# A joined set of new orders in a two-layer decoder trunk: paired u blocks, split first loads, gate products moved, and wide SwiGLU products first

## The chip, the cores and the metric

The kernel runs on one core of one Trainium2 chip. The metric is device time in microseconds for one execution, as the median of several. Five engines work side by side: TensorE (PE in the profile; its weight loads are PEld), VectorE (DVE), ScalarE (ACT), GpSimd (POOL) and SyncE (SP), whose queue issues nearly all loads.

## The reference

Sequence 256, model width 1024, two layers, all in float32. Layer 0 mixes tokens with a gated MLP, layer 1 with an mLSTM. Each mixer is followed by a SwiGLU and by a gated embedding.

```python
def gmlp_mixer(x, w_in, ln_g, ln_b, w_s, b_s, w_out):
    z = jax.nn.gelu(x @ w_in)                 # 1024 -> 2 x 3072
    u, v = jnp.split(z, 2, axis=-1)
    v = layer_norm(v, ln_g, ln_b)             # over 3072, then in 8 groups
    sv = jnp.einsum('gts,bcsgd->bctgd', ws, v) + b_s.T[:, :, None]
    return (u * sv.reshape(B, S, GM_HALF)) @ w_out

def mlstm_mixer(x, ...):
    xm, z = jnp.split(x @ w_in, 2, axis=-1)   # 1024 -> 2 x 2048
    xc = jax.nn.silu(causal_depthwise_conv(xm, conv_w, conv_b))
    q, k, v = (headwise_linear(a, w) for a, w in ((xc, w_q), (xc, w_k), (xm, w_v)))
    gates = jnp.concatenate([q, k, v], axis=-1) @ w_gates + b_gates
    h = mlstm_cell(...)                       # 4 heads of 512, stabilised by running maxima
    h = layer_norm(h, norm_g).reshape(B, S, ML_INNER) + skip * xc
    return (h * jax.nn.silu(z)) @ w_out

def swiglu(x, w_gate, w_up, w_down):          # 1024 -> 2816 -> 1024
    return (jax.nn.silu(x @ w_gate) * (x @ w_up)) @ w_down

for i in range(DEPTH):
    x = layer_norm(ALPHA * x + mixer_i(x), ln1_g[i], ln1_b[i])
    x = layer_norm(ALPHA * x + swiglu(x, ...), ln2_g[i], ln2_b[i])
    x = x + sigmoid(x @ ple_w_gate[i] + ple_b_gate[i]) * (p[i] @ ple_w_proj[i])
```

## The kernel before, in words

**Every product is three.** A float32 operand is split into a high part (a cast to float32r, on ACT) and a low part (the difference, on DVE; both by `split`, L150). A product is then high by high, high by low and low by high. Two forms exist. In the plain form (`mm_feat`, L242, used by `feat_from_x`, L247) a block of 128 features takes 24 products of 256 columns, three per slice of the model width. In the paired form (`feat_pair`, L252) the high and low parts of x stand side by side in `xs`, so one product of 512 columns (a *wide* one) does two of the three, and one of 256 columns (a *narrow* one) the third: eight wide, then eight narrow. A paired result lies in two halves of a PSUM bank, which `pair_sum` (L259) adds: a copy on ACT, then an add on DVE. Before the change the SwiGLU's gate and up blocks are paired, and the gMLP's u blocks and the mLSTM's xm and z blocks are plain.

**Weights.** All weights pass through one list (`weight_plan`, L74) in the order of their use. `weight(...)` (L205) hands out the next one and calls `ahead` (L169), which lets SP load up to 8 weights ahead into four `raw` buffers and casts up to 4 ahead into six `w` buffers (or, for those in `WIDE`, eight `b8` buffers). `EARLY` (L50) names weights that are put into the list next to another one, ahead of their turn, among them the embedding's gates (`pg`) beside blocks of the down projection (`d`). Reading a `w` buffer on TensorE frees it for the cast six later.

**PSUM.** Two pools of four banks: A for accumulators, scores and gates, B for blocks in passing.

**The stages.** Four pairs of loads of x and of the v weights open the program (L342 to L363), with seven warm-up products on TensorE meanwhile. Then come the gMLP's v (six column groups of 512), its u and sv blocks with the output projection three steps behind (L465 to L477), the boundary with layer norm, the SwiGLU (`gate_up`, L529, blocks 4 to 21; the down projection two blocks behind), the boundary and the embedding. Layer 1 follows: in a loop over 16 feature blocks (L770) `xm_block` makes the convolution, `qv_block` q and v, and `s_block` the scores. Then the gate chain (L785 to L840) turns accumulated gate values into exponents. Small transposes on TensorE (`gp`, `cp`) and a broadcast (`gb`) feed a chain of narrow DVE and ACT operations, with z blocks 8 to 11 between. `pv_block` (L844) multiplies scores by values for each head, normalises each head by its own statistics (`num`, `pd`, and the scale by `rsqrt` on POOL) and writes `hn`; z blocks 12 to 15 lie between the heads. `h_block` (L882) transposes `hn` and multiplies by z. The output projection (`Down`, L280; weights `mo`) accumulates into all four A banks: `acc.add` does both token halves of a block, but the last four blocks' second halves are held for the boundary.

The scheduler orders the instructions of each engine from the program's order and its own estimates; each engine then runs its row strictly in order.

## Time and profile before

| | |
|---|---|
| median of 3 runs | 838.34 us (837.59 to 840.28) |
| the profiled execution's own time | 837.17 us |
| its span in the profile | 835.4 us |
| TensorE busy | 824.1 us (99%), 4727 products |
| DVE busy | 608.8 us (73%) |
| ACT busy | 472.5 us (57%) |
| POOL busy | 158.4 us (19%) |
| read from memory | 153.67 MB, 185 GB/s over the span |

In rows of the timeline the first number is the start in microseconds, the second the length, then engine, line, operation, output and inputs by the program's names, partitions by elements, and the count. In brackets stands how long the engine had been idle before it, and what released it. Matmuls are pipelined: neighbours overlap, so the pace of TensorE is read from the differences of starts and not from the lengths.

### The profile page before, as it was taken

The numbers are of one execution on the slowest core, as the hardware profiler recorded it, in microseconds if no ns is written. First come the engines' busy times: TensorE is split into PE (matmuls) and PEld (weight loads), VectorE is DVE, ScalarE is ACT, GpSimd is POOL, SyncE is SP. The second block draws the span as 40 slices with busy tenths as digits, with TensorE's granted clock in tenths as the row PEclk, the third lists the DMA queues.
The fourth block names the chain that finished last, engine by engine and source line by source line (L and its number), as shares of the span: only waits on it lengthen the run. The fifth ranks groups of instructions, "written<-read, shape, count | busy, mean of one in ns | idle before, by whom it ended". The sixth has DMA issues, their size and how long they took to land.

```text
span 835.4 us, 12743 instructions
## 1 busy us (share of the span) xinstructions
PE 824.1 (99%) x4727; PEld 719.6 (86%) x4727; DVE 608.8 (73%) x933; ACT 472.5 (57%) x803; POOL 158.4 (19%) x222
## 2 busy tenths in 40 slices
PE   8999999999999999999999999999999999999997
PEld 5889999998888888888889999898878888888886
DVE  6667996567856666578878998578886666677684
ACT  6556665555544555467347787685544555566522
POOL 1021654443100001800101655230010000000010
PEclk9999999999999999999999999999999999999999
DMA  8885465567286655588234444253646655577601
GB/s 299 294 304 178 143 196 192 177 196 243 102 290 202 188 191 193 164 261 265 80 134 165 140 140 154 95 193 121 209 166 243 206 190 193 187 244 259 202 0 52
DMA packets 44710, 155.55 MB, mean 186 GB/s; under 512 B 5224, under 2 KB 5992, under 8 KB 44648
## 3 DMA queue, kind: packets, MB, share of 16 engines
q1 hardware_dynamic: 44360, 154.47, 56.0%
q8 instruction: 37, 0.61, 0.3%
q10 hardware_dynamic: 288, 0.26, 0.1%
q14 instruction: 25, 0.20, 0.1%
HBM read 153.67 MB, written 1.05 MB: 185 GB/s over the span
## 4 chain that ended last, share of the span: by engine, by line
PE 63%; DVE 5%; DMA 3%; ACT 2%; issue 1%; POOL 1%; DVEq 0%; ACTq 0%; SPq 0%; POOLq 0%
PE pu L255 8%; PE pg L255 8%; PE acc L239 5%; PE acc L238 5%; PE acc L240 5%; PE pu L257 4%; PE pg L257 4%; PE gate L275 2%; PE gate L278 2%; PE gate L276 2%; PE first L275 2%; PE first L278 2%; PE first L276 2%; DVE w L152 2%; DMA raw<-in_ml_wo 1%; PE xmps L243 1%
## 5 line engine op out<-in xcount | busy, mean ns | idle before, releaser
L152 DVE TENSOR_TENSOR w<-raw,w 128x1024 fp32r<-128x1024 f32 (+1 forms) x277 | 337.2, 1225 | 108.6 <-ACT w L152 106.0
L152 ACT CAST w<-raw 128x1024 fp32r<-128x1024 f32 (+1 forms) x276 | 287.3, 1045 | 152.7 <-PE acc L240 50.7
L238 PE MATMUL acc<-w,h 128*128 128x512 f32 x336 | 132.0, 393 | 1.6 <-ACT hn L878 1.0
L239 PE MATMUL acc<-w,h 128*128 128x512 f32 x336 | 131.5, 391 | 0.0
L240 PE MATMUL acc<-w,h 128*128 128x512 f32 x336 | 130.8, 390 | 0.5 <-DVE w L152 0.5
L238 PEld LDWEIGHTS acc<-w,h 128*128 128x128 f32 x336 | 63.2, 188 | 14.5 <-ACT hn L878 1.4
L240 PEld LDWEIGHTS acc<-w,h 128*128 128x128 f32 x336 | 63.1, 188 | 14.5 <-DVE w L152 1.0
L239 PEld LDWEIGHTS acc<-w,h 128*128 128x128 f32 x336 | 63.2, 188 | 11.1 <-DVE h L152 0.3
L255 PE MATMUL pu<-xs,w 128*128 128x512 f32 x288 | 72.3, 393 | 0.0
L255 PE MATMUL pg<-xs,w 128*128 128x512 f32 x288 | 71.8, 391 | 0.0
L255 PEld LDWEIGHTS pg<-xs,w 128*128 128x128 f32 x288 | 53.8, 188 | 11.0
L307 POOL TENSOR_SCALAR ve<-mv 128x1 f32<-128x1 f32 x8 | 6.1, 758 | 294.8 <-DVE mv L327 290.5
L255 PEld LDWEIGHTS pu<-xs,w 128*128 128x128 f32 x288 | 51.5, 188 | 9.3
L244 PE MATMUL ups<-xs,w 128*128 128x256 f32 x192 | 53.7, 280 | 0.0
L243 PE MATMUL ups<-xs,w 128*128 128x256 f32 x192 | 53.6, 279 | 0.0
L245 PE MATMUL ups<-xs,w 128*128 128x256 f32 x192 | 53.6, 279 | 0.0
L442 POOL TENSOR_TENSOR sv<-sv,cf 128x256 f32<-128x256 f32 x24 | 31.1, 1298 | 67.8 <-ACT sv L441 64.0
L257 PEld LDWEIGHTS pg<-xs,w 128*128 128x128 f32 x288 | 38.9, 188 | 3.1
L257 PEld LDWEIGHTS pu<-xs,w 128*128 128x128 f32 x288 | 38.9, 188 | 3.1
L257 PE MATMUL pu<-xs,w 128*128 128x256 f32 x288 | 39.5, 279 | 0.0
L257 PE MATMUL pg<-xs,w 128*128 128x256 f32 x288 | 39.4, 279 | 0.0
L238 PE MATMUL vps<-w,xs 128*128 128x512 f32 x96 | 37.6, 392 | 1.5 <-ACT w L152 0.8
(240 smaller groups left out, 1675.7 us busy)
## 6 DMA issues: line engine op xcount, KB each, us to landing
raw<-in_ffn_g SPq DMA_DIRECT2D x44, 512.0 KB, 3.9
raw<-in_ffn_u SPq DMA_DIRECT2D x44, 512.0 KB, 4.0
raw<-in_ffn_d SPq DMA_DIRECT2D x44, 512.0 KB, 3.4
raw<-in_gm_u SPq DMA_DIRECT2D x24, 512.0 KB, 3.5
raw<-in_gm_wo SPq DMA_DIRECT2D x24, 512.0 KB, 3.4
raw<-in_gm_v SPq DMA_DIRECT2D x23, 512.0 KB, 4.9
raw<-in_ple_gate SPq DMA_DIRECT2D x16, 512.0 KB, 4.5
raw<-in_ml_z SPq DMA_DIRECT2D x16, 512.0 KB, 3.3
```

The costliest lines, as they stand in the source:

```text
L152: return dve.tensor_copy(hi, src) if fast else act.copy(hi, src), sub.tensor_tensor(lo, src, hi.bitcast(F32), ALU.subtract)
L238: pe.matmul(ps, lh, w[:, 0, c], start=start, stop=False)
L239: pe.matmul(ps, ll, w[:, 0, c], start=False, stop=False)
L240: pe.matmul(ps, lh, w[:, 1, c], start=False, stop=stop)
L243: pe.matmul(ps, w[:, 0, c], h, start=start, stop=False)
L244: pe.matmul(ps, w[:, 0, c], l, start=False, stop=False)
L245: pe.matmul(ps, w[:, 1, c], h, start=False, stop=stop)
L255: pe.matmul(ps, w[:, 0, k * P:(k + 1) * P], xs[:, k], start=k == 0, stop=False)
L257: pe.matmul(ps[:, 0], w[:, 1, k * P:(k + 1) * P], xh[:, k, :], start=False, stop=k == KD - 1)
L275: pe.matmul(ps, xh[:, k, TOK[t]], w[:, 0, c], start=k == 0, stop=False)
L276: pe.matmul(ps, xh[:, k, TOK[t]], w[:, 1, c], start=False, stop=False)
L278: pe.matmul(ps, xl[:, k, TOK[t]], w[:, 0, c], start=False, stop=k == KD - 1)
```

## The change

It joins several edits.

- *Start.* The first three v weights (before: the first alone) are loaded and cast in halves. The second half of the first x tile is issued by SP behind the first half weight, not by ACT. Eight warm-up products instead of seven.
- *u blocks.* They take the paired form, with `pair_sum` ahead of the Gelu.
- *SwiGLU.* `feat_pair` is cut in two. In all but the last two blocks the wide products of both factors come first, then the narrow ones of both.
- *Embedding gates.* The early casts of `pg` lie beside down blocks 10 to 15 instead of 13 to 18.
- *xm blocks.* The split of xm comes ahead of the three convolution steps on DVE.
- *Gate chain.* The gate transposes lie within z block 8 (after three of its eight slices), the transposes `cp` and all broadcasts `gb` within z block 10, in two banks. z block 12 is done there too, and one activation covers five blocks.
- *Heads.* The square of the reciprocal is taken early, and the variance's scale and the epsilon are one DVE operation; one POOL operation goes. Four weights are cast ahead of the last head. z blocks 13 to 15 follow heads 0 to 2, and none follows head 3.
- *Output projection.* Blocks 0 and 1 do their first token halves one after the other, then their second halves.

```diff
-WARM = 7
+WARM = 8
...
+LAST = 2
+GATES_STEP = 3
...
-EARLY |= {("d", l, 13 + k): ("pg", l, k) for l in range(2) for k in range(6)}
+EARLY |= {("d", l, 10 + k): ("pg", l, k) for l in range(2) for k in range(6)}
...
-    return key[0] in ("g", "u") and len(key) == 3 and key[-1] >= 4
+    return key[0] in ("g", "u") and len(key) == 3 and key[-1] >= 4 or key[0] == "u" and len(key) == 2
...
-            for c in HALF if at["load"] == 0 else [slice(0, n)]:
+            for c in HALF if at["load"] < 3 else [slice(0, n)]:
                 sp.dma_start(t[:, c], ap[:, c])
+                if at["load"] == 0 and c.start == 0:
+                    second_x()
...
-                for c in () if key[0] == "bdv" else HALF if i == 0 else [slice(0, n)]:
+                for c in () if key[0] == "bdv" else HALF if i < 3 else [slice(0, n)]:
...
-    def feat_pair(ps, w):
+    def feat_pair_high(ps, w):
 
         for k in range(KD):
             pe.matmul(ps, w[:, 0, k * P:(k + 1) * P], xs[:, k], start=k == 0, stop=False)
+
+    def feat_pair_low(ps, w):
         for k in range(KD):
             pe.matmul(ps[:, 0], w[:, 1, k * P:(k + 1) * P], xh[:, k, :], start=False, stop=k == KD - 1)
...
     def u_block(f):
-        ps = bank("B", [P, S], "ups")
-        feat_from_x(ps, weight("u", f))
+        ps = bank("B", [P, 2, S], "ups")
+        feat_pair(ps, weight("u", f))
         us[f] = tl("s", [P, S], name="u")
-        act.activation(us[f], ps, AF.Gelu_apprx_tanh)
+        pair_sum(us[f], ps)
+        act.activation(us[f], us[f], AF.Gelu_apprx_tanh)
...
-            pg = bank("B", [P, 2, S], "pg")
-            feat_pair(pg, weight("g", l, f))
+            pg, pu = bank("B", [P, 2, S], "pg"), bank("B", [P, 2, S], "pu")
+            wg = weight("g", l, f)
+            feat_pair_high(pg, wg)
+            if f < NF - LAST:
+
+                wu = weight("u", l, f)
+                feat_pair_high(pu, wu)
+                feat_pair_low(pg, wg)
+            else:
+                feat_pair_low(pg, wg)
+                wu = weight("u", l, f)
+                feat_pair_high(pu, wu)
             pair_sum(s, pg)
             act.activation(s, s, AF.Silu)
-            pu = bank("B", [P, 2, S], "pu")
-            feat_pair(pu, weight("u", l, f))
+            feat_pair_low(pu, wu)
             pair_sum(y, pu)
...
-            act.activation(y, ps, AF.Identity, bias=par[:, f, 4:5], scale=par[:, f, 3:4])
-            for j in (1, 2, 3):
-                dve.scalar_tensor_tensor(y[:, j:], ps[:, :S - j], par[:, f, 3 - j:4 - j], y[:, j:], ALU.mult, ALU.add)
...
+            act.activation(y, ps, AF.Identity, bias=par[:, f, 4:5], scale=par[:, f, 3:4])
             split(xm[0][:, 0, :], xm[0][:, 1, :], ps)
+            for j in (1, 2, 3):
+                dve.scalar_tensor_tensor(y[:, j:], ps[:, :S - j], par[:, f, 3 - j:4 - j], y[:, j:], ALU.mult, ALU.add)
...
-            z8 = z_mm(8)
...
+            z8 = z_mm(8, (GATES_STEP, transpose_gates))
...
+            gbs = [bank("A", [P, 2, 2, P], "gb") for _ in range(2)]
+            z = z_mm(10, (GATES_STEP, transpose_cols))
...
-            act.activation(sz[1][:, 0:4, :], sz[1][:, 0:4, :], AF.Silu)
+            z_copy(*z_mm(12))
+            act.activation(sz[1][:, 0:5, :], sz[1][:, 0:5, :], AF.Silu)
...
-            dve.tensor_tensor(rs, mv[:, :, 1], dn, ALU.mult)
-            dve.tensor_tensor(rs, rs, dn, ALU.mult)
-            rsqrt(rs, rs, 2)
+            for t in range(2):
+                dve.tensor_scalar(rs[:, t:t + 1], mv[:, t, 1:2], dn2[:, t:t + 1], EPS, ALU.mult, ALU.add)
+            pool.tensor_tensor(rs, rs, mhalf[:, :2], ALU.pow)
...
+            if h == NH - 1:
+                ahead(LOAD_AHEAD, 4)
             pv_block(h)
-            z_act(*z_mm(12 + h))
+            if h < NH - 1:
+                z_act(*z_mm(13 + h))
...
-                acc.add(f, hs.pop(f), weight("mo", f, casts=1 if f >= NI - 2 else None))
+                block = (f, hs.pop(f), weight("mo", f, casts=1 if f >= NI - 2 else None))
+                if f == 0:
+                    first = block
+                elif f == 1:
+
+                    for t in range(2):
+                        for b, h2, w in (first, block):
+                            acc.mm(b, t, h2, w)
+                else:
+                    acc.add(*block)
```

`transpose_gates` and `transpose_cols` hold the transposes that stood in line before, and the second also the four `gb` products; `feat_from_x` calls them after three slices.

More of the change, by code (lines that the diff above doesn't have):

```diff
@@ L350, in trunk @@
         if i == 0:
-            for k in range(2):
-                act.dma_start(t[:, k, :], a["xT"][i, :, k, :])
+            act.dma_start(t[:, 0, :], a["xT"][i, :, 0, :])
+            second_x = lambda: sp.dma_start(xr[0][:, 1, :], a["xT"][0, :, 1, :])
+            xr.append(t)
         else:
             sp.dma_start(t, a["xT"][i])
+            xr.append(t)
         ahead(1 + i, int(i == 0))
-        xr.append(t)
     make_identity(nc, ident)
@@ L687, in transpose_z, with z_mm @@
                 act.copy(sz[0][:, 0:4, TOK[t]], tp)
-        def z_mm(f):
+        def z_mm(f, between=(None, None)):
             ps = bank("B", [P, S], "zps")
-            feat_from_x(ps, weight("z", f, casts=2 if f > 10 else None))
+            feat_from_x(ps, weight("z", f, casts=2 if f > 10 else None), between)
             return f, ps
@@ L794, in mlstm, with transpose_gates @@
         with tc.manual_schedule(engines={mybir.EngineType.Activation}):
-            z8 = z_mm(8)
             gp = bank("A", [4, 2, S], "gp")
-            for i in range(2):
-                for t in range(2):
-                    pe.transpose(gp[:, i, TOK[t]], gacc[:, t, 4 * i:4 * i + 4], ident)
+            def transpose_gates():
+                for i in range(2):
+                    for t in range(2):
+                        pe.transpose(gp[:, i, TOK[t]], gacc[:, t, 4 * i:4 * i + 4], ident)
+            z8 = z_mm(8, (GATES_STEP, transpose_gates))
             dve.tensor_scalar(fs, gp[:, 1, :], gbias[:, 1:2], None, ALU.add)
@@ L810, in mlstm, with transpose_cols @@
             z_copy(*z8)
-            z = z_mm(9)
+            z_copy(*z_mm(9))
             cp = bank("A", [P, 4, 4], "cp")
-            for i, src in enumerate((ai, ex)):
-                for t in range(2):
-                    pe.transpose(cp[:, 2 * i + t, :], src[:, TOK[t]], ident[:4, :4])
+            def transpose_cols():
+                for i, src in enumerate((ai, ex)):
+                    for t in range(2):
+                        pe.transpose(cp[:, 2 * i + t, :], src[:, TOK[t]], ident[:4, :4])
+                for h in range(NH):
+                    pe.matmul(gbs[h // 2][:, h % 2], selH[:, h, :], G, start=True, stop=True)
+            gbs = [bank("A", [P, 2, 2, P], "gb") for _ in range(2)]
+            z = z_mm(10, (GATES_STEP, transpose_cols))
             dve.tensor_copy(cols[:, 0:2, :], cp[:, 0:2, :])
@@ L819, in mlstm @@
             for h in range(NH):
-                gb = bank("A", [P, 2, P], "gb")
-                pe.matmul(gb, selH[:, h, :], G, start=True, stop=True)
-                if h in (0, 3):
+                gb = gbs[h // 2][:, h % 2]
+                if h == 3:
                     z_copy(*z)
-                    z = z_mm(10 if h == 0 else 11)
+                    z = z_mm(11)
                 gm = tl("s", [P, 2, P], name="gm")
@@ L864, in pv_block @@
             dve.reciprocal(dn, dn)
+            dn2 = tl("c", [P, 2], name="dn2")
+            dve.tensor_tensor(dn2, dn, dn, ALU.mult)
             st = tl("c", [P, 2, 6], name="hst")
@@ L870, in pv_block @@
             rs = tl("c", [P, 2], name="hrs")
-            dve.tensor_tensor(rs, mv[:, :, 1], dn, ALU.mult)
-            dve.tensor_tensor(rs, rs, dn, ALU.mult)
-            rsqrt(rs, rs, 2)
+            for t in range(2):
+                dve.tensor_scalar(rs[:, t:t + 1], mv[:, t, 1:2], dn2[:, t:t + 1], EPS, ALU.mult, ALU.add)
+            pool.tensor_tensor(rs, rs, mhalf[:, :2], ALU.pow)
             dve.tensor_tensor(rs, rs, dn, ALU.mult)
@@ L907, in mlstm @@
             for f in range(4 * h, 4 * h + 4):
-                acc.add(f, hs.pop(f), weight("mo", f, casts=1 if f >= NI - 2 else None))
+                block = (f, hs.pop(f), weight("mo", f, casts=1 if f >= NI - 2 else None))
+                if f == 0:
+                    first = block
+                elif f == 1:
+                    for t in range(2):
+                        for b, h2, w in (first, block):
+                            acc.mm(b, t, h2, w)
+                else:
+                    acc.add(*block)
         return acc
```

7 lines of the change are left out of this document (6 added, 1 removed).

## The prediction

> **What bounds the kernel now.** I read the page's busy table first, then the busy time by stretches, then the timeline at every place where TensorE stood still. The first three lines are the page's, the rest are stretches of the program (bounds, length, then busy time and count of PE, PEld, DVE, ACT and POOL, granted clock, DMA share, GB/s).
>
> ```profile
> span 835.4 us, 12743 instructions
> ## 1 busy us (share of the span) xinstructions
> PE 824.1 (99%) x4727; PEld 719.6 (86%) x4727; DVE 608.8 (73%) x933; ACT 472.5 (57%) x803; POOL 158.4 (19%) x222
> ...
> 80.00:92.00 12.00, 11.94 (x102) 11.74 (x101) 11.36 (x18) 8.26 (x15) 6.04 (x5) 1.00 0.45 144
> 92.00:212.00 120.00, 119.72 (x775) 108.69 (x774) 88.14 (x122) 66.47 (x112) 54.81 (x61) 1.00 0.61 196
> 240.00:400.00 160.00, 160.00 (x846) 137.41 (x845) 105.03 (x146) 88.56 (x146) 19.34 (x30) 1.00 0.67 215
> 522.00:575.00 53.00, 50.22 (x356) 45.79 (x355) 38.14 (x105) 39.79 (x77) 12.53 (x23) 1.00 0.33 114
> 575.00:612.00 37.00, 36.13 (x167) 29.43 (x165) 30.79 (x47) 19.02 (x25) 0.00 (x0) 1.00 0.72 241
> ...
> 800.00:835.40 35.40, 31.14 (x168) 26.72 (x167) 22.86 (x43) 8.45 (x15) 3.02 (x4) 0.98 0.08 31
> ```
>
> TensorE is the bound: 824.1 of 835.4 us, at full clock. In the gMLP and SwiGLU stretches it does not stop at all, so time can leave only in two ways: the same products issued in a cheaper order, or the few stops, which lie at the start and between 522 and 612 us. They are small: 11.3 us of idle in all, of which 4.3 us lie in the last stretch, behind the last product.
>
> **Cadence, SwiGLU.** One steady block of the first layer on TensorE, in order of time (start, length, then the group). Differences between the starts are what counts, since neighbouring products overlap.
>
> ```profile
> 318.03 1.98 PE L255 MATMUL pg<-xs,w 128*128 128x512 f32 x8
> 319.86 1.10 PE L257 MATMUL pg<-xs,w 128*128 128x256 f32 x8
> 320.79 2.01 PE L255 MATMUL pu<-xs,w 128*128 128x512 f32 x8
> 322.64 1.10 PE L257 MATMUL pu<-xs,w 128*128 128x256 f32 x8
> 323.57 0.40 PE L238 MATMUL acc<-w,h 128*128 128x512 f32 x1
> ```
>
> Eight wide products take 1.83 us when they follow the wide products of the down projection (319.86 less 318.03), but 1.85 us when they follow narrow ones (322.64 less 320.79). Eight narrow ones take 0.93 us either way. So a passage from narrow to wide costs about 0.02 us; the passage back can't be told apart in rows of ten nanoseconds, and I put it at 0.01 us. The change takes out one such pair, 0.03 us, per block. TensorE's row before, at a steady block (pg is the gate factor, pu the up factor, acc the down projection):
>
> ```order
> L240 MATMUL acc<-w,h 128x512
> L255 MATMUL pg<-xs,w 128x512 x8
> L257 MATMUL pg<-xs,w 128x256 x8
> L255 MATMUL pu<-xs,w 128x512 x8
> L257 MATMUL pu<-xs,w 128x256 x8
> L238 MATMUL acc<-w,h 128x512
> ```
>
> and now, at the same place:
>
> ```order
> L244 MATMUL acc<-w,h 128x512
> L262 MATMUL pg<-xs,w 128x512 x8
> L262 MATMUL pu<-xs,w 128x512 x8
> L266 MATMUL pg<-xs,w 128x256 x8
> L266 MATMUL pu<-xs,w 128x256 x8
> L242 MATMUL acc<-w,h 128x512
> ```
>
> The up factor's wide products moved ahead of the gate factor's narrow ones. That is 16 blocks in each of two layers: 32 x 0.03 = **1.0 us** (0.6 to 1.3). It has no cover to lose, because TensorE itself is the path. The moved step needs the up weight 0.93 us sooner and keeps the gate weight 1.85 us longer; a weight is cast into the buffer of the one six before it, two blocks ahead of its use, and DVE and ACT are busy 66% and 55% of this stretch, so I cost both at nothing. If that cover were gone, each block would wait up to 0.93 us.
>
> [...]
>
> **Cadence, gMLP's u blocks.** Before, a block is 24 narrow products; the change makes it eight wide and eight narrow, the form of pg.
>
> ```profile
> 125.30 0.28 PE L243 MATMUL ups<-xs,w 128*128 128x256 f32 x1
> ...
> 128.10 0.64 PE L435 MATMUL svps<-ws,vn 128*128 128x256 f32 x4
> ```
>
> A u block takes 2.80 us after a down projection; pg, in that position, 2.76 (320.79 less 318.03), and the passage into narrow products ahead of it goes too: 0.04 to 0.05. 24 x 0.045 = **1.1 us** (0.9 to 1.3). It adds a PSUM copy on ACT and an add on DVE per block, like those of pg:
>
> ```profile
> 304.43 0.37 ACT L260 COPY s<-pg 128x256 f32<-128x256 f32 x1 [1.66 <-PE pg L257]
> ...
> 304.83 0.42 DVE L261 TENSOR_TENSOR s<-s,pg 128x256 f32<-128x256 f32 x1 [0.81 <-ACT s L260]
> ```
>
> From 92 to 212 us DVE would rise from 88.1 to about 88.1 + 20 x 0.42 = 96.5 of 120 us: hidden. From 80 to 92 us it is already at 11.36 of 12, and four more adds make 13.0; there it may cost up to 1 us, but there the new order puts two of the normalisations of v behind the first sv, so I take nothing.
>
> **The start.** The page's memory traffic in 40 slices of 20.9 us, then the first lines of work:
>
> ```profile
> GB/s 299 294 304 178 143 196 192 177 196 243 102 290 202 188 191 193 164 261 265 80 134 165 140 140 154 95 193 121 209 166 243 206 190 193 187 244 259 202 0 52
> ```
>
> ```profile
> 0.79 0.85 SPq L175 DMA_DIRECT2D raw<-in_gm_v  x2
> ...
> 1.24 3.15 PE L346 MATMUL warm<-warm 128*128 128x512 bf16 x7 [1.24 <-DVE warm L343]
> ...
> 5.01 0.50 PE L238 MATMUL vps<-w,xs 128*128 128x512 f32 x1 [0.62 <-DVE w L152]
> ...
> 5.56 0.62 ACT L152 CAST w<-raw 128x512 fp32r<-128x512 f32 x1
> ...
> 8.29 1.04 ACT L152 CAST w<-raw 128x1024 fp32r<-128x1024 f32 x1 [1.58 <-DMA raw<-in_gm_v]
> ...
> 9.38 0.50 PE L238 MATMUL vps<-w,xs 128*128 128x512 f32 x1 [0.83 <-ACT w L152]
> ```
>
> TensorE waits 0.83 us for the second weight, which landed whole at 8.29 and was cast whole in 1.04. The change halves loads and casts of the second and third weight: half a cast is 0.62 us, and the first half lands 256 KB sooner, which at the first slice's 299 GB/s is an estimated 0.85 us. So it is ready by 8.1 to 8.9 us instead of 9.33, and the later weights land when they did. I take **1.0 us** (0 to 1.3; below that, three more issues on SP of 0.43 us each (0.85 over two) might push the second weight back by as much). The eighth warm-up product adds 0.45 (3.15 over seven) to 4.39 and ends before 5.01: nothing.
>
> **The last xm block.** Between 522 and 530 us:
>
> ```profile
> 523.50 0.47 DVE L708 SCALAR_TENSOR_TENSOR conv<-xmps,par,conv 128x253 f32<-128x253 f32 x1
> ...
> 524.00 0.37 ACT L152 CAST xm<-xmps 128x256 fp32r<-128x256 f32 x1 [2.25 <-DVE conv L708]
> ...
> 525.32 0.43 DVE L152 TENSOR_TENSOR xm<-conv,xm 128x256 fp32r<-128x256 f32 x1 [0.49 <-ACT xm L152]
> ...
> 525.66 0.42 DVE L152 TENSOR_TENSOR q<-qps,q 128x256 fp32r<-128x256 f32 x1
> ...
> 526.13 0.39 PE L243 MATMUL qps<-xm,bdm 128*128 128x256 f32 x1 [1.45 <-DVE q L152]
> ```
>
> ACT stands 2.25 us behind DVE's third convolution step, and TensorE 1.45 us behind DVE's low part of q. DVE's row before, and now, from the last block's convolution to that low part of q (w is a weight's low part, xm the two split tiles):
>
> ```order
> L708 SCALAR_TENSOR_TENSOR conv_5468<-xmps_5438,par_75,conv_5468 128x254
> L152 TENSOR_TENSOR w_5620<-raw_5357,w_5620 128x1024
> L708 SCALAR_TENSOR_TENSOR conv_5468<-xmps_5438,par_75,conv_5468 128x253
> L736 TENSOR_TENSOR vsum_5481<-vsum_5481,vps_5487 128x136
> L790 COPY sel_5612<-ident_70 4x512
> L152 TENSOR_TENSOR xm_5473<-xmps_5438,xm_5473 128x256
> L152 TENSOR_TENSOR xm_5474<-conv_5468,xm_5474 128x256
> L152 TENSOR_TENSOR q_5499<-qps_5495,q_5499 128x256
> ```
>
> ```order
> L740 SCALAR_TENSOR_TENSOR conv_5331<-xmps_5301,par_75,conv_5331 128x254
> L762 TENSOR_TENSOR vsum_5344<-vsum_5344,vps_5350 128x136
> L740 SCALAR_TENSOR_TENSOR conv_5331<-xmps_5301,par_75,conv_5331 128x253
> L816 COPY sel_5475<-ident_70 4x512
> L154 TENSOR_TENSOR w_5484<-raw_5220,w_5484 128x1024
> L154 TENSOR_TENSOR xm_5333<-conv_5331,xm_5333 128x256
> L154 TENSOR_TENSOR q_5362<-qps_5358,q_5362 128x256
> ```
>
> The weight's low part moved behind the convolution, and the split of xm ahead of it. The same work stands before q, but ACT gets its convolution sooner and DVE's 0.49 us of idling for ACT goes. I take half the wait, **0.7 us** (0 to 1.45).
>
> **Gates, and the start of the output projection.** Here the change moves the gate transposes into z block 8, the next ones into block 10, and z block 12 ahead of the value products.
>
> ```profile
> 533.08 0.36 PE L243 MATMUL zps<-xs,w 128*128 128x256 f32 x1
> ...
> 538.26 0.28 PE L815 MATMUL cp<-ident,gt 4*128 4x4 f32 x2 [0.27 <-DVE gt L806]
> ...
> 538.95 0.41 DVE L808 TENSOR_TENSOR gt<-gt 4x256 f32<-4x256 f32 x1
> ```
>
> The gate transposes end and z resumes at 533.08; the chain on DVE and ACT that they feed ends at 538.95 + 0.41, 6.3 us later. Now 48 z products lie between, 48 x 0.117 (2.80 us over 24) = 5.6 us: a wait of about 0.6 us replaces one of 0.27 and several passages between z and gate products. I take nothing (from 0.5 saved to 0.6 lost).
>
> ```profile
> 565.36 0.37 PE L243 MATMUL zps<-xs,w 128*128 128x256 f32 x1
> ...
> 568.26 1.04 PE L887 MATMUL tp<-ident,hn 128*128 128x128 f32 x8
> 569.05 0.48 PE L238 MATMUL acc<-w,h 128*128 128x512 f32 x1
> ...
> 572.64 1.45 ACT L878 ACTIVATE hn<-num,nb,hrs 128x512 f32<-128x512 f32 x2 [1.12 <-DVE nb L876]
> ...
> 573.47 0.50 PE L238 MATMUL acc<-w,h 128*128 128x512 f32 x1 [0.99 <-ACT hn L878]
> ```
>
> TensorE waits 0.99 us for ACT to read the last head's PSUM bank: 573.47 less 565.36 is 8.1 us after that head's products. Before, a z block (2.9 us), transposes (0.8) and 14 products (3.2) covered 6.9 of it. Now the z block is gone from here; 24 products of the first tokens (24 x 0.229, the 1.83 over eight, = 5.5) and two sets of transposes (1.6) cover 7.1. The row before is on the last products ahead of the wait, with tiles numbered (acc_6117 and acc_6118 are the first tokens, acc_6119 waits); the row now stands beneath it.
>
> ```order
> L240 MATMUL acc_6118<-w_6157,h_6029 128x512
> L238 MATMUL acc_6117<-w_6160,h_6040 128x512
> L239 MATMUL acc_6117<-w_6160,h_6040 128x512
> L238 MATMUL acc_6119<-w_6089,h_6023 128x512
> L239 MATMUL acc_6119<-w_6089,h_6023 128x512
> ```
>
> ```order
> L244 MATMUL acc_5990<-w_5949,h_5938 128x512
> L925 MATMUL tp_6090<-ident_70,hn_5854 128x128 x4
> L925 MATMUL tp_6107<-ident_70,hn_5854 128x128 x4
> L242 MATMUL acc_5989<-w_6029,h_6001 128x512
> L242 MATMUL acc_5991<-w_5879,h_5915 128x512
> ```
>
> Four weights' first-token products now stand ahead of the waiting one, instead of two and a part. The chain itself loses one step on POOL and one on DVE, but DVE has more of the h blocks to do within it. I take nothing (1.0 saved to 1.3 lost).
>
> **The end of the output projection.**
>
> ```profile
> 609.47 0.50 PE L238 MATMUL acc<-w,h 128*128 128x512 f32 x1 [0.34 <-ACT w L152]
> ...
> 610.73 0.50 PE L240 MATMUL acc<-w,h 128*128 128x512 f32 x1 [0.53 <-DVE w L152]
> ```
>
> 0.87 us is lost to the last casts. DVE is at 30.8 of 37 us here; the change casts four of these weights ahead of the last head, so DVE starts with less. I take **0.5 us** (0 to 0.9). The gates of the embedding, cast three down blocks sooner, wait for nothing now: zero.
>
> **The sum.** 1.0 + 1.1 + 1.0 + 0.7 + 0.5 = 4.3 us. The profiled execution took 837.17 us (1.7 us around its span) and would take 832.9; it lies 1.2 us under the median of the runs shown, 838.34, which becomes **834.0**. About 0.3% (2.5 us) is what a measurement here can tell from no change.
>
> **Rivals.** *The waits only move.* Every stop but the start's lies in one stage where DVE has little room; if q, the gates and the accumulators wait as long as before, the cadence is left, 2.1 us, 836.2. For it: two of my terms there are already zero. Against: ACT's 2.25 us behind the convolution has lost its reason. Chance 0.16. *Order is free.* If the 1.85 us belongs to pu and not to its place, SwiGLU gives nothing, and a u block may cost 1.85 + 0.93 = 2.78, which is 24 x 0.02 = 0.5 instead of 1.1: 4.3 - 1.0 - 0.6 = 2.7, 835.6. Against: pg and pu have the same operands, shapes and pools, and differ in nothing but place. Chance 0.06. [...] *DVE becomes the bound of the u stage.* If the added 0.42 us per u block is exposed, 24 x 0.42 = 10.1 less 4.3, so 5.8 slower: 844.1. It decides where DVE reaches the whole of a step; the 80 to 92 stretch says yes, the 120 us after it (80% with the adds) say no. Chance 0.04. The forecast keeps 0.74.
>
> **Numbers.** All good ends together give 831, all bad ones 838.4; ends do not fall together, so the range is 831.2 to 836.8. Faster by over 0.3%: 0.74 and part of the second rival, 0.77; within it 0.18; slower 0.05.
>
> **What would show it.** Right: 3.65 us for sixteen wide products in a row, 2.75 us u blocks, a first wait of the v weights under 0.3 us, qps waiting under 0.8, about 4536 products. Wrong: TensorE waiting for DVE's u adds between 76 and 95 us, or over 2 us between the last num and the second tokens' acc.

## The result, and the profile after

The changed kernel takes 833.48 us, the median of four runs (832.62 to 833.73); the kernel before took 838.36 beside it, median of four (837.59 to 840.28). The ratio is 0.9933, with a 95% interval of 0.9914 to 0.9951: faster by 0.5 to 0.9%. The forecast was 834.0 us, between 831.2 and 836.8. The profiled execution took 833.73 us, its span is 831.9 (before: 837.17 and 835.4).

The first lines are the page's busy table of the changed kernel; then the same stretches of the program as before (bounds, length, busy time and count of PE, PEld, DVE, ACT and POOL, granted clock, DMA share, GB/s).

```profile
span 831.9 us, 12439 instructions
## 1 busy us (share of the span) xinstructions
PE 822.6 (99%) x4536; PEld 712.2 (86%) x4536; DVE 616.9 (74%) x963; ACT 477.5 (57%) x827; POOL 160.1 (19%) x218
```

```profile
92.00:212.00 120.00, 119.22 (x630) 102.08 (x629) 96.86 (x144) 75.73 (x134) 48.05 (x60) 1.00 0.60 193
...
522.00:575.00 53.00, 51.00 (x351) 46.82 (x350) 39.65 (x105) 35.88 (x71) 14.74 (x18) 0.97 0.40 134
575.00:612.00 37.00, 37.00 (x168) 30.65 (x168) 31.16 (x49) 19.98 (x28) 0.00 (x0) 1.00 0.65 222
```

TensorE is the bound as before. It has 191 products fewer on record (pairing the u blocks takes away 24 x 8 = 192), and between 575 and 612 us it no longer stops. New is a granted clock of 0.97 between 522 and 575 us, which was 1.00.

Where the 3.5 us of span went is read from the starts of the first product of each stage, in the two timelines. Each row is one trace against one; the experiments show which rows repeat:

| stage on TensorE | before, us | after, us | difference |
|---|---|---|---|
| start, to the first u product | 73.34 | 72.45 | -0.90 |
| u stage, to the boundary's first product | 145.79 | 144.96 | -0.83 |
| boundary, to the first pg product | 26.66 | 26.66 | 0 |
| SwiGLU, layer 0 | 160.48 | 159.97 | -0.51 |
| embedding, z and xm, to the last xm block | 110.52 | 110.62 | +0.09 |
| end of the xm stage, to z block 8 | 13.06 | 13.48 | +0.42 |
| gates and heads, to the output projection | 39.19 | 39.86 | +0.67 |
| output projection | 48.17 | 45.63 | -2.54 |
| boundary, to the first pg product | 26.66 | 27.13 | +0.47 |
| SwiGLU, layer 1 | 160.48 | 159.97 | -0.52 |
| end | 31.06 | 31.20 | +0.14 |

**Cadence.** A steady SwiGLU block and a steady u block of the changed kernel, on TensorE (start, length):

```profile
316.06 1.98 PE L262 MATMUL pg<-xs,w 128*128 128x512 f32 x8
317.87 1.98 PE L262 MATMUL pu<-xs,w 128*128 128x512 f32 x8
319.69 1.10 PE L266 MATMUL pg<-xs,w 128*128 128x256 f32 x8
320.63 1.09 PE L266 MATMUL pu<-xs,w 128*128 128x256 f32 x8
321.56 0.40 PE L242 MATMUL acc<-w,h 128*128 128x512 f32 x1
...
123.66 1.98 PE L262 MATMUL ups<-xs,w 128*128 128x512 f32 x8
125.48 1.10 PE L266 MATMUL ups<-xs,w 128*128 128x256 f32 x8
126.41 0.64 PE L451 MATMUL svps<-ws,vn 128*128 128x256 f32 x4
```

Sixteen wide products in a row take 319.69 - 316.06 = 3.63 us (before 1.83 + 1.85), the sixteen narrow ones 1.87. The u block takes 126.41 - 123.66 = 2.75 us (before 2.80). The forecast named 3.65 and 2.75.

**Start.** The second weight is now cast in halves. Its first product starts at 7.47 instead of 9.38 us, and waits 0.41 instead of 0.83:

```profile
6.80 0.62 ACT L154 CAST w<-raw 128x512 fp32r<-128x512 f32 x1 [1.97 <-DMA raw<-in_gm_v]
...
7.47 0.50 PE L242 MATMUL vps<-w,xs 128*128 128x512 f32 x1 [0.41 <-ACT w L154]
```

**The end of the xm stage.** All engines between 521 and 525 us:

```profile
521.41 2.26 POOL L154 TENSOR_TENSOR vn<-vsum,vn 128x256 fp32r<-128x256 f32 x1
521.54 1.21 DVE L154 TENSOR_TENSOR w<-raw,w 128x1024 fp32r<-128x1024 f32 x1
...
523.01 0.40 DVE L154 TENSOR_TENSOR q<-qps,q 128x256 fp32r<-128x256 f32 x1
...
523.47 0.39 PE L247 MATMUL qps<-xm,bdm 128*128 128x256 f32 x1 [1.03 <-DVE q L154]
...
524.53 0.46 POOL L769 CAST q<-wx 128x16 fp32r<-128x16 f32 x3
...
524.77 0.39 PE L783 MATMUL s<-q,xm 128*128 128x264 f32 x1 [0.68 <-POOL q L769]
```

One wait of 1.45 us became two of 1.03 and 0.68. Counted from the first product of the last xm block, this q product starts after 8.82 us instead of 9.34, so q did come half a microsecond sooner. But from it to the first product of the scores it now takes 1.30 us instead of 0.46, and that is more than was won. POOL's low part of vn took 2.26 us (0.72 for the one at 525.15) and stands ahead of the columns of q that POOL writes for the scores. In the kernel before it came behind the first of them:

```profile
525.66 0.20 POOL L743 CAST q<-wx 128x16 fp32r<-128x16 f32 x1
525.82 0.74 POOL L152 TENSOR_TENSOR vn<-vsum,vn 128x256 fp32r<-128x256 f32 x1
```

**The gates.** TensorE behind the `cp` transposes, and the granted clock in stretches of 4 us (PE busy, clock, DMA share, GB/s):

```profile
535.93 0.28 PE L846 MATMUL cp<-ident,gt 4*128 4x4 f32 x2 [0.28 <-DVE gt L837]
536.07 1.97 PE L848 MATMUL gb<-gt,sel 4*128 4x256 f32 x8
537.97 0.46 PE L247 MATMUL zps<-xs,w 128*128 128x256 f32 x1
538.23 0.42 PE L248 MATMUL zps<-xs,w 128*128 128x256 f32 x1
...
541.43 0.34 PE L248 MATMUL zps<-xs,w 128*128 128x256 f32 x1
541.61 0.28 PE L249 MATMUL zps<-xs,w 128*128 128x256 f32 x1
```

```profile
534.00:538.00 4.00, 3.72 (x26) 1.00 0.02 4
538.00:542.00 4.00, 4.00 (x22) 0.57 0.86 253
542.00:546.00 4.00, 4.00 (x37) 1.00 0.88 314
```

The wait for the gate chain is 0.28 us, less than the 0.6 of the forecast. But behind the burst of all four `gb` products the z products start 0.213 us apart instead of 0.117, fifteen of them until 541.43: 15 x 0.096 = 1.4 us lost at a granted clock of 0.50 (538.5 to 541.5 us; called the half clock below), without an idle moment. No row of the profile before showed that.

**The output projection.** TensorE no longer idles for `hn` (0.99 before) or for casts (0.34 and 0.53). The rows are TensorE's at the place of the old wait and at the start of the projection, SP's load of the last weight `mo` (after, then before), and its cast on ACT after:

```profile
567.99 0.48 PE L242 MATMUL acc<-w,h 128*128 128x512 f32 x1
...
573.55 1.04 PE L925 MATMUL tp<-ident,hn 128*128 128x128 f32 x8
574.35 0.89 PE L242 MATMUL acc<-w,h 128*128 128x512 f32 x2
```

```profile
600.66 0.33 SPq L177 DMA_DIRECT2D raw<-in_ml_wo  x1
```

```profile
603.82 0.33 SPq L175 DMA_DIRECT2D raw<-in_ml_wo  x1
```

```profile
604.58 1.05 ACT L154 CAST w<-raw 128x1024 fp32r<-128x1024 f32 x1 [1.47 <-DMA raw<-in_ml_wo]
```

### The profile page after: what moved, and what is told of

It is laid out like the page before. It is cut to its first block, busy times and chain, and to the rows that moved or that the text cites. A ratio compares the mean times of both kernels' runs of the same rounds, so it can differ in the third digit from the quotient of the medians.

```text
span 831.9 us, 12439 instructions
## 1 busy us (share of the span) xinstructions
PE 822.6 (99%) x4536; PEld 712.2 (86%) x4536; DVE 616.9 (74%) x963; ACT 477.5 (57%) x827; POOL 160.1 (19%) x218
## 4 chain that ended last, share of the span: by engine, by line
PE 69%; DVE 3%; POOL 1%; ACT 1%; issue 1%; DMA 0%; DVEq 0%; ACTq 0%
PE pu L262 8%; PE pg L262 8%; PE acc L242 7%; PE acc L243 7%; PE acc L244 7%; PE pg L266 4%; PE pu L266 4%; PE gate L288 2%; PE gate L291 2%; PE first L289 2%; PE gate L289 2%; PE first L291 2%; PE first L288 2%; PE tp L328 1%; PE xmps L247 1%; PE zps L247 1%
## 5 line engine op out<-in xcount | busy, mean ns | idle before, releaser
L262 PEld LDWEIGHTS pu<-xs,w 128*128 128x128 f32 x288 | 53.8, 188 | 11.1
L273 ACT COPY s<-pg 128x256 f32<-128x256 f32 x36 | 13.4, 372 | 76.0 <-PE pg L266 76.0
L274 DVE TENSOR_TENSOR s<-s,pg 128x256 f32<-128x256 f32 x36 | 15.1, 420 | 47.9 <-ACT s L273 47.8
L262 PE MATMUL ups<-xs,w 128*128 128x512 f32 x192 | 47.7, 391 | 0.0
L262 PEld LDWEIGHTS ups<-xs,w 128*128 128x128 f32 x192 | 35.7, 188 | 7.2
L458 POOL TENSOR_TENSOR sv<-sv,cf 128x256 f32<-128x256 f32 x24 | 23.7, 988 | 73.8 <-ACT sv L457 70.0
```

Of the source, the lines that this page charges most:

```text
L262: pe.matmul(ps, w[:, 0, k * P:(k + 1) * P], xs[:, k], start=k == 0, stop=False)
L274: dve.tensor_tensor(o, o, ps[:, 0], ALU.add)
L458: pool.tensor_tensor(sv, sv, cf.unsqueeze(1).to_broadcast([P, 2, P]), ALU.add)
```

## The experiments

Each edits the kernel before or the changed one, and is read by its stages in one profile. Only e23_joined and e24_joined_z_behind ran more than once; every other time below is of a single run, and not all ran on the same chip. Stages of the same code repeat from kernel to kernel, which shows how far one trace can be trusted.

**e1_swiglu_order: the SwiGLU order alone, on the kernel before.**

```diff
-            feat_pair(pg, weight("g", l, f))
...
-            feat_pair(pu, weight("u", l, f))
...
+                feat_pair_high(pu, wu)
+                feat_pair_low(pg, wg)
...
+            feat_pair_low(pu, wu)
```

> The kernel before, with the new SwiGLU order alone (wide products of both factors first, in all but the last two blocks). Theory, passages cost: each SwiGLU stretch of TensorE, from the first pg product to the first product of the boundary that follows, shortens by 0.5 us (before: 160.5 us in each layer, changed kernel: 160.0), 16 blocks x 0.03, so about 1.0 us in all; sixteen wide products in a row take 3.65 us instead of 1.83 + 1.85. Rival, the order is free: the two stretches stay at 160.5 us and the 0.5 us that the changed kernel saved in each came from the casts of the embedding's gates, which lie elsewhere in it.

The layer 1 stretch on TensorE, first pg product to first boundary product, was

```profile
647.47 2.09 PE L256 MATMUL pg<-xs,w 128*128 128x512 f32 x8
...
807.42 0.39 PE L239 MATMUL pps<-w,pt 128*128 128x512 f32 x1
```

159.95 us against 160.48: the 0.53 that the changed kernel gains, from the order alone. In layer 0 it took 160.57, since three products from 398.6 us on, which came late for the last h, lost 0.57 at its end; no kernel with the gates of the embedding cast three blocks sooner shows that. Passages cost here, 0.53 us over 16 blocks; the order is not free. The run as a whole took 840.19 us, 2.8 more than the kernel before beside it: the half clock stood over its last `gb` products and behind them, for some 6.8 us until 547.7, though they lie as before the change (two passes, five z products, six passes):

```profile
538.00:542.00 4.00, 4.00 (x19) 0.86 0.27 90
542.00:546.00 4.00, 4.00 (x20) 0.50 0.90 319
546.00:550.00 4.00, 4.00 (x26) 0.79 1.00 377
```

**e2_u_pairs: the u blocks alone, on the kernel before.**

```diff
-        ps = bank("B", [P, S], "ups")
-        feat_from_x(ps, weight("u", f))
+        ps = bank("B", [P, 2, S], "ups")
+        feat_pair(ps, weight("u", f))
```

> The kernel before, with the paired u blocks alone. Theory: a u block falls from 2.80 to 2.75 us between 92 and 212 us, so 20 to 24 blocks give 1.0 to 1.3 us, of which the wait for the last h of the gMLP at about 212 us gives back 0.5 (0.28 us before, 0.78 in the changed kernel), because the last three sv blocks go at the pace of POOL, ACT and DVE and not of TensorE: 0.6 to 0.9 us net up to the first product of the boundary. Rival: the 0.78 us wait comes with another part of the change (the casts are ordered anew), then it stays at 0.28 and the whole 1.1 to 1.3 us arrive.

The u stage took 144.97 us, 0.82 less than before, with a wait for the last h:

```profile
211.60 0.49 PE L238 MATMUL acc<-w,h 128*128 128x512 f32 x1 [0.77 <-ACT h L152]
```

So far the theory. But the wait does not come with the pairing: of the ten traces with paired u blocks two have it (0.78 and 0.77), and in eight it is 0.04 us or nothing and the stage takes 143.6 to 144.1 us, on average 143.82; of the four with plain ones only the profile before has it (0.28), the other three took 144.97 to 144.98. Without it pairing gives 144.97 - 143.82 = 1.15 us, the forecast's term. What makes the wait come and go with the same code stays open. (The run took 837.95 us. Its gain went elsewhere: v products stood 0.427 us apart, half the pace, until 10.2 us, and the first head's products waited 0.97 us for `plo`, which no other kernel with that stage shows.)

**e3_spread_gb: the `gb` products apart, on the changed kernel.**

```diff
+            z = z_mm(10, {GATES_STEP: transpose_cols, GATES_STEP + 3: lambda: broadcast(1)})
...
-                if h == 3:
+                if h == 2:
                     z_copy(*z)
-                    z = z_mm(11)
+                    z = z_mm(11, {1: lambda: broadcast(2), 4: lambda: broadcast(3)})
```

> The changed kernel, with its four gb products (eight passes of 0.216 us each) not in one burst but one by one, behind slices 4 and 7 of z block 10 and slices 1 and 4 of z block 11. Theory, the granted clock falls because of the burst: for more than 1.7 us TensorE works with 4 of its 128 rows alone, and then 16 products of z take 0.213 us instead of 0.117; spread, the clock stays at 1.00 from 530 to 548 us and 1.5 us are saved (16 x 0.096) between the cp transposes and the first num product. Rival, the clock falls by its own timing or because of the 0.28 us wait and the transposes ahead: then the slow stretch is there again, at the same place or some microseconds off.

The clock stayed at 1.00. From the `cp` transposes to the first num product TensorE took 11.31 us against 11.62: only 0.3 saved, because each lone `gb` costs two passages, 0.18 to 0.20 us in and 0.19 out. The run took 832.38 us.

**e4_xm_order: the split of xm behind the convolution again, on the changed kernel.**

```diff
-            split(xm[0][:, 0, :], xm[0][:, 1, :], ps)
             for j in (1, 2, 3):
                 dve.scalar_tensor_tensor(y[:, j:], ps[:, :S - j], par[:, f, 3 - j:4 - j], y[:, j:], ALU.mult, ALU.add)
+            split(xm[0][:, 0, :], xm[0][:, 1, :], ps)
```

> The changed kernel, with the split of xm behind the three convolution steps again, as before the change. The prediction's theory: the split ahead of the convolution frees ACT from 2.25 us of waiting and saves 0.7 us at the end of the xm stage, so undoing it costs 0.7. The theory that the result suggests: the changed kernel lost 0.47 us between the last xmps product and z block 8 (waits of 1.03 us for q and 0.68 for s where one of 1.45 stood), since with the split first the convolution, and with it q, comes one DVE operation of 0.43 us later; undoing it gives 0.4 to 0.5 us back and the waits read about 1.45 again. Rival: the two orders cost the same and the 0.47 us come from the weights' low parts that the scheduler put in between; then the stage from the last xmps product to z block 8 stays at 13.5 us.

From the last xm block to z block 8 it took 13.06 us, as before the change, 0.42 less than the changed kernel, and one wait stands there again:

```profile
521.83 0.39 PE L247 MATMUL qps<-xm,bdm 128*128 128x256 f32 x1 [1.45 <-DVE q L154]
```

The old order gives 13.03 to 13.07 us in nine traces (e10_z8_early, with a z block more in the stage, is left out), the new one 13.48 or 13.49 in three of its four (14.68 in e9_scale_back, with the half clock). In all fourteen traces the two halves part in the same way: up to the q product that waits it takes 9.31 to 9.34 us with the old order and 8.82 or 8.83 with the new, and from there to the scores 0.46 or 0.47 and 1.30. So the edit won 0.5 us for q and lost 0.8 to the wait for POOL; it cost 0.4 us where 0.7 was forecast as a gain. The run took 831.30 us.

**e8_z12_back and e9_scale_back: who made the gain of the output projection.** On the changed kernel, z blocks 12 to 15 behind the heads, and the old scale:

```diff
-            z_copy(*z_mm(12))
...
-            if h < NH - 1:
-                z_act(*z_mm(13 + h))
+            z_act(*z_mm(12 + h))
```

```diff
-            for t in range(2):
-                dve.tensor_scalar(rs[:, t:t + 1], mv[:, t, 1:2], dn2[:, t:t + 1], EPS, ALU.mult, ALU.add)
-            pool.tensor_tensor(rs, rs, mhalf[:, :2], ALU.pow)
+            dve.tensor_tensor(rs, mv[:, :, 1], dn, ALU.mult)
+            dve.tensor_tensor(rs, rs, dn, ALU.mult)
+            rsqrt(rs, rs, 2)
```

> The changed kernel, with z blocks 12 to 15 behind heads 0 to 3 again (none ahead of the heads, one activation over four blocks). Theory, the z block's place made the gain in the output projection: with z block 15 behind the last head its cast and its products stand ahead of the output projection's weights, so the two waits for casts at the end (0.34 and 0.53 us before the change, none in the changed kernel) and the wait for the last head's PSUM bank (0.99 before, none after) come back in part, 1.0 to 2.0 us between the last num product and the boundary, measured without the 2.8 us of the z block itself. Rival, the scale chain of the heads made it (one POOL and one DVE operation less): then nothing comes back here, and run e9_scale_back shows it.

> The changed kernel, with the heads' scale worked out as before the change (variance times the reciprocal twice, then epsilon and power on POOL). Theory of the z block: TensorE's waits between the last num product and the boundary stay under 0.4 us in all, as in the changed kernel. Rival, the scale chain made the gain: a wait for hn of about 0.4 to 1.0 us stands at the second tokens' first product of the output projection.

The projection took 45.94 and 46.46 us (changed kernel 45.63, before 48.17). The waits for `hn`, e8's and then e9's:

```profile
572.70 0.50 PE L242 MATMUL acc<-w,h 128*128 128x512 f32 x1 [0.16 <-ACT hn L915]
```

```profile
574.38 0.50 PE L242 MATMUL acc<-w,h 128*128 128x512 f32 x1 [0.66 <-ACT hn L914]
```

The scale chain bears more of that wait than the z block; but the casts wait in neither, so neither edit had removed that. Both theories miss the larger half. The wait also goes with the clock: e3_spread_gb, e11_gb_float32r and e23_joined have the changed kernel's heads and a whole clock in the gate stage, and there `hn` waits 0.40 or 0.41 us and the projection takes 46.1 to 46.5; with the half clock ahead of it (the changed kernel and e4_xm_order) there is no such wait and it takes 45.6 or 45.7. (833.01 and 833.83 us.)

**e19_gates_only and e20_z12_only: one edit each, on the kernel before.**

```diff
+            z8 = z_mm(8, (GATES_STEP, transpose_gates))
...
+            z = z_mm(10, (GATES_STEP, transpose_cols))
```

```diff
+            z_copy(*z_mm(12))
...
-            z_act(*z_mm(12 + h))
+            if h < NH - 1:
+                z_act(*z_mm(13 + h))
```

> The kernel before, with the edits of the gate stage alone (gate transposes within z block 8, the cp transposes and all four gb products in one burst within z block 10). Theory, one of several moves is enough for the casts: two more weights are cast ahead of the last head's statistics (the low parts of weights that stand ahead of them in the row of DVE: 190 instead of 188), so the waits for casts near the end of the output projection (0.34 and 0.53 us before) go, and the time from the last num product to the boundary falls from 53.7 to about 52.4 us while the wait for hn (0.99) stays. Rival, the casts come early only with z block 12 ahead of the heads: then 53.5 us or more remain. The clock: with all gb products in one burst it falls again behind them (1.5 to 3 us of full-speed time lost); if it does not, the burst alone is not sufficient.

> The kernel before, with z blocks 12 to 15 one place forward alone (12 ahead of the heads, none behind the last). Theory, the same casts come early (191 low parts ahead of the last head's statistics instead of 188): the waits for casts at the end of the output projection go, and the time from the last num product to the boundary, which held 2.8 us of z products before, falls from 53.7 to 53.7 - 2.8 - 1.2 = 49.7 us, or to 48.6 if the wait for hn goes too because more first-token products stand ahead of it. Rival, without its z block the last head's normalisation is exposed: a wait for hn of 1 to 3 us, and 50.7 us or more.

With the gate edits alone the projection took 46.59 us, 1.58 less than before, and only `hn` waits:

```profile
571.28 0.50 PE L239 MATMUL acc<-w,h 128*128 128x512 f32 x1 [0.84 <-ACT hn L891]
```

The whole run took 833.30 us, as little as the changed kernel, with neither its u blocks nor its SwiGLU order. That does not make the gate edits the whole change: of the 3.8 us by which its span is shorter than that of the profile before, 1.58 lie in the projection and 0.59 in the gates and heads, while 1.7 lie in the start, the u stage and the stage up to the last xm block, whose code it does not touch. It is one run, with a whole clock.

With z block 12 alone (841.03 us, half clock included) it took 48.17, nothing gained. Nothing there waits for `hn` any more (0.51 us of such a wait now stand among the heads), but the casts do:

```profile
613.33 0.50 PE L238 MATMUL acc<-w,h 128*128 128x512 f32 x1 [0.93 <-ACT w L152]
...
614.59 0.50 PE L240 MATMUL acc<-w,h 128*128 128x512 f32 x1 [0.53 <-DVE w L152]
```

So the number of weights cast ahead (188 before, 190 in e19, 191 in e20) does not decide it. What goes with the waits in all fourteen traces is when SP issues the load of the last `mo` weight, counted from the projection's first product: after 34.2 to 35.7 us in the four kernels with the old gate stage, all of which wait for casts, and after 30.3 to 33.4 in the ten with the new one, none of which does. In the changed kernel it is 600.66 - 567.99 = 32.7, before 603.82 - 569.05 = 34.8. In both, that load starts as a weight's low part ends on DVE (SP waits 1.4 us for it, before 1.1), which frees one of the four `raw` buffers. That the load decides is argued and not shown, since no run moved it alone; how the gate edits bring it forward stays open.

And e19's clock stayed whole, with the very burst that the changed kernel has:

```profile
538.00:542.00 4.00, 4.00 (x35) 1.00 0.91 262
542.00:546.00 4.00, 4.00 (x26) 1.00 0.94 359
```

The burst is not enough by itself.

**e10_z8_early: a z block against the wait for q.** On the changed kernel with e4's order.

```diff
-Z_AFTER_XM = {3: 4, 7: 5, 11: 6, 15: 7}
+Z_AFTER_XM = {3: 4, 7: 5, 11: 6, 15: 7, 16: 8}
...
+            z9 = z_mm(9, (GATES_STEP, transpose_gates))
...
+            if h < NH - 2:
+                z_act(*z_mm(14 + h))
```

> The changed kernel with the split of xm behind the convolution (as in e4_xm_order) and one z block drawn forward: block 8 comes between the steps 16 and 17 of the xm loop, blocks 9 to 13 take the places of 8 to 12, and 14 and 15 follow heads 0 and 1. Theory, the wait of 1.45 us for q at the end of the xm stage is only a lack of other products: with 24 z products (2.8 us) ahead of it, it is gone, and the time from the last xmps product to the first gate transpose grows by 1.2 to 1.6 us instead of 2.8. Price: head 2 has no z block behind it, and a wait of 0 to 1.0 us may come at the last head's num products or at the second tokens' acc. Rival, DVE and ACT are the bound of that end: then the wait only moves to the next q or s product, and the stage grows by the whole 2.8 us.

It does not answer its question: the wait of 1.45 us stands at 522.31, ahead of the place where the z block came. Its price is clear, over twice my bound: without a z block behind head 2, the last head's products wait.

```profile
565.52 0.50 PE L888 MATMUL num<-vn,phi 128*128 128x512 f32 x1 [2.27 <-ACT hn L916]
```

Behind that wait, too, the clock fell (0.67 between 565 and 569 us). The run took 835.61 us.

**e11_gb_float32r: a shorter burst.** On the changed kernel with e4's order.

```diff
+            split(g2[:, 0], g2[:, 1], G)
...
-                    pe.matmul(gbs[h // 2][:, h % 2], selH[:, h, :], G, start=True, stop=True)
+                    for i in range(2):
+                        pe.matmul(gbs[h // 2][:, h % 2], selH[:, h, :], g2[:, i], start=i == 0, stop=i == 1)
```

> The changed kernel with the split of xm behind the convolution (as in e4_xm_order), and the broadcasts gb as two float32r products each (high and low part of G, split on ACT and DVE) in place of one float32 product of two passes. They still use 4 of 128 rows, but the burst takes 8 x 0.117 = 0.9 us instead of 8 x 0.216 = 1.7. Theory, the clock falls when too little of TensorE is at work within some microseconds: with 0.8 us less of such work it stays at 1.00 between 530 and 548 us, which saves 0.8 us of burst and 1.6 us of half-clock products against e4_xm_order. Rival, the clock falls after any stretch of products with 4 rows, or by its own timing: then granted clocks under 0.9 stand again behind the burst, and only 0.8 us are saved. The split puts about 0.8 us on the gate chain, so a wait for G of up to 0.8 us may stand ahead of the burst.

The clock stayed at 1.00, there was no wait for G, and from `cp` to the first num product it took 9.43 us (e4_xm_order 11.65): 2.2 saved of the 2.4 that were expected. A later wait, for ACT's copy of z, took part of it back:

```profile
547.13 0.38 PE L247 MATMUL zps<-xs,w 128*128 128x256 f32 x1 [0.74 <-ACT sz L723]
```

The run took 831.35 us, no better than e4_xm_order's 831.30 on another chip.

**e23_joined and e24_joined_z_behind: towards a faster kernel.** Both have e4's and e11's edits. The first also has

```diff
-                if h == 3:
+                if h == 2:
                     z_copy(*z)
...
-        dve.tensor_copy(selH, ident[:4, 0:4].unsqueeze(2).to_broadcast([4, 4, P]))
+        pool.tensor_copy(selH, ident[:4, 0:4].unsqueeze(2).to_broadcast([4, 4, P]))
```

and the second z blocks 12 to 15 behind the heads, as in e8.

> The changed kernel with the split of xm behind the convolution (as in e4_xm_order), gb in float32r (as in e11_gb_float32r), the copy of z block 10 out of PSUM one head earlier on ACT (against the wait of 0.74 us for that copy which stood ahead of z block 13 in e11_gb_float32r), and the constant selH made by POOL instead of DVE (0.41 us of DVE inside the chain that q waits for at the end of the xm stage). Theory: against the changed kernel's 833.5 us, 0.4 for the xm order, 0.8 for the burst and 1.6 for the clock, 0.4 for selH less 0.4 for the longer gate chain: 830.5 us (829.5 to 831.5), granted clocks of 0.998 to 1.000 in every run where the changed kernel had 0.996 to 0.998. Rival, the clock falls by its own timing: clocks of 0.995 to 0.997 in some runs, and 832 us.

> The changed kernel with the split of xm behind the convolution (as in e4_xm_order), gb in float32r (as in e11_gb_float32r), and z blocks 12 to 15 behind heads 0 to 3 (as in e8_z12_back); selH and the copy of z block 10 as in the changed kernel. In e8_z12_back TensorE lost about 3.2 us to the half clock behind gb and only 0.16 us to the wait for hn; in e11_gb_float32r and e23_joined, whose clock stayed whole, 0.7 to 1.0 us went to a wait among the heads and 0.4 to hn. Theory: e8_z12_back's 833.0 us less 3.2 (clock), 0.8 (burst) and 0.4 (xm order), plus 0.5 to 1.0 because 4.5 us of z products now have to cover the first head's exponents: 829.4 us (828.5 to 830.5). Rival, the exponents' chain is the bound once the clock is whole: a wait of 2 us or more ahead of the first num product and 831 us, no better than e23_joined.

e23_joined took 831.59 us (six runs, 830.51 to 832.47) against 837.36 beside it, ratio 0.993 (0.9914 to 0.9945); e24 832.00 (831.87 to 832.89) against 837.83, ratio 0.993 (0.9916 to 0.9943). Their medians are lower than the changed kernel's 833.48, but the intervals of the ratios fall together with its own (0.9914 to 0.9951): neither is shown to be faster than it. Both lie above the ranges expected for them. In both profiles the clock is whole through the gate stage, but TensorE waits elsewhere: in e23 0.98 us for the first h of the projection and 0.40 for `hn`, with q's 1.45 unchanged, so selH on DVE was no part of it. In e24 the rival came true:

```profile
540.86 0.50 PE L890 MATMUL num<-vn,phi 128*128 128x512 f32 x1 [0.82 <-ACT phi L154]
...
542.94 0.50 PE L892 MATMUL num<-vn,plo 128*128 128x512 f32 x1 [1.34 <-POOL plo L154]
```

The first head's exponents come 2.2 us late. In e8_z12_back the half clock, and in e19_gates_only the longer burst and a chain without the split of G, may have left them the time; no run separates these.

## Why the prediction was right, and where its steps were not

The forecast for the profiled execution was 832.9 us; it took 833.73. The total is right within a microsecond, and that is partly luck: the term for the xm block is wrong by 1.1 us and the output projection by 2.0 the other way, and what was lost in the gates and elsewhere, 1.4 us, was not in the sum. The mechanism was right for the SwiGLU, the u blocks and the start. Two of the forecast's signs of being right did not come: the first wait of the v weights is 0.41 us and not under 0.3, and `qps` waits 1.03 and not under 0.8.

- **SwiGLU order, 1.0: right**, 0.51 + 0.52, and 0.53 in e1 by itself. The rival "order is free" falls: the same 32 products took 0.03 us less in another order (0.51 us over 16 blocks).
- **u blocks, 1.1: right in size**, 1.15 between traces without the wait at the end; 0.83 in this pair of profiles, because that wait was 0.78 here and 0.28 before. It is not shown to be a price of the change. The forecast said that TensorE does not stop at all in the gMLP stretch; the 0.28 us were in its own row, 119.72 of 120. DVE stayed hidden (96.9 of 120 us, forecast 96.5), so the third rival falls.
- **Start, 1.0: right**, 0.90 in this pair; over all traces the first u product comes at 72.15 us (nine with the edit, 71.84 to 72.53) against 73.42 (five without, 72.94 to 73.79), 1.3 us.
- **The last xm block, 0.7: wrong in sign**, -0.42. The step "ACT gets its convolution sooner" held, and "half the wait" nearly: q came 0.51 us sooner. The step that failed is the price of what stands behind q, which was put at nothing. I read DVE's rows alone and did not ask about POOL, whose columns of q the scores need too; from q to the scores it took 0.84 us longer.
- **Gates, 0: just outside its range (0.6 lost at most)**, -0.67. The forecast weighed the wait (0.28 came for 0.6) and the passages, not the clock, which took 1.4 us. Without that, by this reckoning, the stage would have gained 0.8; e19, with a whole clock, gained 0.59.
- **Start of the output projection, 0, and its end, 0.5: undersized**, 2.54 together. Counted between starts, the wait for `hn` had cost 1.15 + 0.11 us rather than the 0.99 of idling, of which 0.16 + 0.11 are left. Those for casts went whole, 0.51 + 0.11 + 0.70 + 0.11 between starts. I had set the end at 0.5 for weights cast ahead of the last head; e20 has more of them cast ahead and waits still, and e19 shows that the gate edits alone end these waits, with the last load 3.4 us sooner (2.1 in the changed kernel). About half a microsecond of the 2.54 seems to have been paid for in the gate stage: with the same heads and a whole clock the projection took 46.1 to 46.5 us and waited 0.4 for `hn`.
- Another 0.7 us was lost where nothing was forecast: 0.47 in the second boundary (26.66 us in most traces, 26.8 to 27.4 in five), 0.14 at the end, 0.09 in between. Its cause was not looked for.
- The forecast's own bounds add up to 830.6 and 838.7 us, not to 831 and 838.4; nothing hung on it.

"The waits only move" was half true: in the xm stage and the gates they did, 1.1 us worse than before, and the projection gave back twice as much.

## What to carry to other kernels

Read a wait between starts, not by its idle time, and ask for each engine in the chain, the small copies on GpSimd included, what the new order puts in front of it. A wait for a cast near a stage's end can hang on edits in an earlier stage; look at when its load could start, and at what freed the buffer for it. And before you believe a gain of a microsecond from one pair of profiles, look at the same stage in other traces: here one wait and one clock step, which came and went with the same code, were as large.

## What the hardware did that was not expected

TensorE's granted clock fell to 0.50 in the middle of a busy stretch. In seven of the ten traces whose `gb` products are float32 passes close together (4 of 128 rows at work, 0.216 us each), z products behind them started 0.213 us apart and lost 1.3 to 2.4 us; the half clock lasted some 3.4 us in the changed kernel and 6.8 in e1_swiglu_order. With the passes spread (one trace) or halved in time (three) none did; but two of the five runs of e24_joined_z_behind had a granted clock of 0.997 and took 832.81 and 832.89 us, the other three 0.999 and 831.87 to 832.00, so a fall in runs without a trace is not excluded. The same code fell in some runs and not in others (e1_swiglu_order yes, e2_u_pairs no), and over eleven runs of the kernel before on one chip the three with a granted clock of 0.995 to 0.996 took 839.8 to 840.4 us, the eight with 0.997 to 1.000 took 836.2 to 837.9. The fall behind the waits of 1.03 and 0.68 us in e9_scale_back gave a second such step in one run:

```profile
520.00:524.00 4.00, 2.29 (x16) 0.94 0.41 135
524.00:528.00 4.00, 4.00 (x25) 0.64 0.00 0
```

What makes the clock fall is not shown. TensorE was not idle ahead of it: in the changed kernel it was busy for 3.72 of 4.00 us between 534 and 538 us, 1.93 of that with the `gb` products of four rows. That these bring it on is a guess: behind the same burst e19_gates_only kept a clock of 1.00, and no run changed the number of rows alone. Since the whole burst left it whole there, the clock of 1.00 in e11_gb_float32r, behind a shorter one, does not show that run's theory of the clock.
